# A two-layer decoder trunk: branch b's gate units computed in pairs, branch a's moved to the attention's end, one head pair's values kept in the rotary tables' tiles

## The chip, the cores and the metric

The kernel runs on one core of a Trainium2 chip. The metric is device time in microseconds (us) of one execution, as the median of a few runs. The core's engines are TensorE (PE, matmuls), VectorE (DVE), ScalarE (ACT), GpSimd (POOL) and SyncE (SP); POOL and SP issue most of the DMA transfers here. L12 is line 12 of the kernel.

## The reference

Each of two layers normalises the input, projects it to 6660 columns, runs three attention branches (a: forgetting attention, 4 heads; b: three dilated bands, 6 heads with rotary; c: a window of 128 with sinks, 6 query heads and 2 key heads with rotary), and merges them with gates:

```python
h = rmsnorm(x, norm_g[layer])
u = jnp.einsum('bsd,dc->bsc', h, w_in[layer])
(qa, ka, va, fa, za, qb, kb, vb, zb, qc, kc, vc, zc, ga, gb, gc) = jnp.split(u, offsets, axis=-1)
...
ya = ya.reshape(b, seq, A_W) * jax.nn.silu(za)        # and yb, yc likewise
...
merged = (jax.nn.sigmoid(ga) * jnp.einsum('bsc,cd->bsd', ya, w_br_a[layer])
          + jax.nn.sigmoid(gb) * jnp.einsum('bsc,cd->bsd', yb, w_br_b[layer])
          + jax.nn.sigmoid(gc) * jnp.einsum('bsc,cd->bsd', yc, w_br_c[layer]))
x = x + jnp.einsum('bsd,de->bse', merged, w_out[layer])
```

The sequence is 512 tokens, the model width 1024, a head 64 wide; a branch is 256 (a) or 384 (b, c) wide, two or three head pairs. A last normalisation follows.

## The kernel before

Activations lie as [128 channels x 512 tokens], weights stream from HBM. Every float32 operand is split in a high and a low part (`xh`, `xl`; `wh`, `wl`), and a product is three matmuls, high by high, high by low and low by high (`mm3`, L130 to L132). A weight chunk comes as a raw float32 tile, ACT makes or copies the parts (L1133, L1139), and a subtraction by DVE or POOL, or a DMA that accumulates (L1140), gives the low part.

**One layer** runs: value, query, key and z projections; an attention loop h = 0 to 16; a few gate units; input sums; pairs of gate units; the output projection (`o_item` in layer 0, `last_projection` in layer 1).

**The attention loop** issues, in iteration h: the transposes of head h-1 (`t_item`, L503), the units of slot a<h>, the value product of head h-1 (`pv_item`), the scores of head h+1 (`s_item`, L438 and L439), then the units of slot b<h>. The dictionary `plan` says which units stand in the slots. The products of scores and transposes go into four PSUM banks (`att`), given out in turn. For heads below 10 the scores take three banks and the transposes three; from head 10 on two and two. A bank of scores is read by the masked reduction on DVE (L472), a bank of transposes by ACT (L528) and DVE (L529). Rotary needs a swap of halves by a DMA from tile to tile on SP's queue; DVE waits for it at L353.

**A gate unit M(br, i)** (`m_item`, br 0, 1, 2 for branch a, b, c, i a block of 128 output channels) is the gate projection of its block (8 channel blocks, 24 matmuls of 512 columns) and the branch product (2 or 3 head pairs, 6 or 9 matmuls of 512 columns). Behind it DVE multiplies by the norm (L632), ACT takes tanh (L633), DVE multiplies gate and product (L639, L642) and, for b and c, adds it to the merged tile (L643).

**A pair** (`pair_steps`) computes two neighbouring gate units at once by a Strassen-Winograd scheme: seven products of a quarter (12 matmuls of 256 columns each; the products 2 to 5 by sums of inputs, `SH`, `SL`, and of raw weights), two branch products, and a chain of small operations (`e1`, `c11`, `e5`, `e2`, `c12`, `c22`, `c21`) that copies, adds, gates and merges the two units. The sums of the inputs are made once a layer at the attention's end (`sums_load` on SP's queue, L594; `sums`, L601 to L611); `x` is loaded again for it.

**Order.** A tile scheduler puts the instructions of each engine in order by priority, from the order in which the code gives them; `urgent` raises it. Instructions on one engine run in that order, and a DMA waits on its queue with all behind it. `raw_slots` names the tiles for the raw weights of the pairs: query and key tiles (`qk`, 12 buffers) up to pair (2,0), then y2 to y9. `y0` to `y9` hold the values of head pairs 0 to 5, two tiles each (pair 5 in y0 and y1 again); `va` tiles hold pairs 6 and 7. In layer 1 the last pair and the projection behind it stand in the order of the code.

## Time and profile before

| | us |
|---|---|
| three runs | 881.23, 884.04, 881.29 (median 881.29) |
| the profiled execution, own time | 884.22 |
| its span, first to last instruction | 882.5 |
| PE busy | 865.5 (98%) |
| DVE busy | 567.9 (64%) |
| ACT busy | 510.4 (58%) |
| POOL busy | 440.5 (50%) |
| layer 0: attention iterations 5 to 10 | 133.30 to 228.40 |
| layer 0: last value product ends, first pair starts | 282.2, 305.17 |
| layer 1: first pair starts | 736.10 |

The granted TensorE clock is 0.994 of full speed over the span. Busy shares are averages over the span; a busy PE is counted from the modelled ends of overlapping matmuls, so what a matmul costs is read from the distance of two starts.

### The profile page before, as it was taken

What the parts mean: (1) busy time and instruction counts of PE and PEld (TensorE: products, weight loads), DVE (VectorE), ACT (ScalarE), POOL (GpSimd) and SP (SyncE); (2) the same over time, 40 slices, a digit from 0 to 9 for tenths busy, and PEclk for the clock granted to TensorE, in tenths of its full rate; (3) what the DMA queues carried; (4) which work ended last, traced back from release to release, by engine and by line L of the source; (5) the groups of instructions that cost most, each with busy time, mean ns of one, the idle gap of its engine ahead of it and who ended that gap; (6) DMA issues with size and microseconds to landing.
All of it is one profiled execution on the core that took longest, in us unless ns stands there. A gap on an engine that the chain in (4) does not pass through costs nothing.

```text
span 882.5 us, 14401 instructions
## 1 busy us (share of the span) xinstructions
PE 865.5 (98%) x4866; PEld 750.1 (85%) x4866; DVE 567.9 (64%) x1242; ACT 510.4 (58%) x1072; POOL 440.5 (50%) x570
## 2 busy tenths in 40 slices
PE   9999999999999999999999999999999999999995
PEld 6988888888888889987888888888888888999994
DVE  7446788577576767752124658967685858687633
ACT  7477567565655655554335856666465756556541
POOL 5354576655444254566654446666444434544301
PEclk9999999999999999999999999999999999999997
DMA  9697768978989799999997886888899897998413
GB/s 303 142 207 141 161 142 168 190 144 189 199 182 228 193 185 247 205 200 284 250 233 156 174 164 149 153 168 172 158 205 193 186 223 158 226 247 183 160 48 111
DMA packets 97082, 163.83 MB, mean 186 GB/s; under 512 B 12144, under 2 KB 26864, under 8 KB 97008
## 3 DMA queue, kind: packets, MB, share of 16 engines
q0 software_dynamic: 71424, 121.70, 69.2%
q1 hardware_dynamic: 25440, 41.20, 14.2%
q8 instruction: 38, 0.62, 0.3%
q14 instruction: 36, 0.29, 0.1%
q10 hardware_dynamic: 144, 0.01, 0.0%
HBM read 153.43 MB, written 4.19 MB: 179 GB/s over the span
## 4 chain that ended last, share of the span: by engine, by line
PE 76%; issue 7%; POOL 5%; DMA 5%; DVE 3%; ACT 2%; SPq 0%; POOLq 0%; DVEq 0%; ACTq 0%
PE mm L131 17%; PE mm L130 17%; PE mm L132 17%; PE att L130 3%; PE att L131 3%; PE att L132 3%; PE pv L549 3%; PE att L503 3%; POOL wl L1140 3%; POOL wh L1110 2%; PE att L439 2%; PE att L438 2%; PE att L234 1%; PE att L235 1%; PE att L233 1%
## 5 line engine op out<-in xcount | busy, mean ns | idle before, releaser
L1140 POOL DMA_DIRECT2D wl<-in_wpk_dram x248 | 224.7, 925 | 185.8 <-ACT wl L1139 157.0
L1110 POOL DMA_DIRECT2D wh<-in_wpk_dram x248 | 169.6, 693 | 175.4 <-PE mm L132 130.2
L1139 ACT ACTIVATE wl<-wh 128x512 fp32r<-128x512 f32 (+3 forms) x248 | 148.3, 602 | 141.7 <-PE mm L132 113.2
L130 PE MATMUL mm<-xh,wh 128*128 128x512 f32 x544 | 217.6, 400 | 0.0
L131 PE MATMUL mm<-xl,wh 128*128 128x512 f32 x544 | 214.5, 394 | 0.0
L132 PE MATMUL mm<-xh,wl 128*128 128x512 f32 x544 | 214.4, 394 | 0.0
L132 PEld LDWEIGHTS mm<-xh,wl 128*128 128x128 f32 x544 | 102.2, 188 | 24.1
L130 PEld LDWEIGHTS mm<-xh,wh 128*128 128x128 f32 x544 | 102.3, 188 | 22.2
L131 PEld LDWEIGHTS mm<-xl,wh 128*128 128x128 f32 x544 | 102.3, 188 | 22.1
L474 ACT ACTIVATE P<-P,ng 128x256 f32<-128x256 f32 (+3 forms) x128 | 67.0, 525 | 24.9 <-DVE ng L472 24.4
L130 PE MATMUL mm<-y,wh 128*128 128x512 f32 (+1 forms) x132 | 49.9, 378 | 1.2 <-ACT y L711 1.2
L529 DVE TENSOR_TENSOR PL<-att,PH 128x512 fp32r<-128x512 f32 (+2 forms) x84 | 46.1, 598 | 7.0 <-ACT PH L528 7.0
L131 PE MATMUL mm<-y,wh 128*128 128x512 f32 (+1 forms) x132 | 50.1, 379 | 0.3 <-DVE y L712 0.3
L132 PE MATMUL mm<-y,wl 128*128 128x512 f32 (+1 forms) x124 | 47.5, 383 | 0.0
L130 PE MATMUL att<-xh,wh 128*128 128x256 f32 x144 | 40.7, 282 | 0.0
L492 DVE TENSOR_SCALAR P<-P,den 128x256 f32<-128x256 f32 (+3 forms) x128 | 39.8, 376 | 1.0
L132 PE MATMUL att<-xh,wl 128*128 128x256 f32 x144 | 40.4, 281 | 0.0
L131 PE MATMUL att<-xl,wh 128*128 128x256 f32 x144 | 40.4, 281 | 0.0
L528 ACT CAST PH<-att 128x512 fp32r<-128x512 f32 (+2 forms) x84 | 38.8, 526 | 1.3 <-PE att L503 0.6
L439 PE MATMUL att<-qk,qk 128*128 128x256 f32 (+2 forms) x128 | 36.9, 308 | 0.0
L503 PE MATMUL att<-ident,P 128*128 128x128 f32 x284 | 36.2, 272 | 0.0
L438 PE MATMUL att<-qk,qk 128*128 128x256 f32 (+2 forms) x128 | 36.1, 308 | 0.0
(260 smaller groups left out, 2034.8 us busy)
## 6 DMA issues: line engine op xcount, KB each, us to landing
wh<-in_wpk_dram POOLq DMA_DIRECT2D x196, 256.0 KB, 4.7
wl<-in_wpk_dram POOLq DMA_DIRECT2D x196, 256.0 KB, 5.2
y<-in_wpk_dram SPq DMA_DIRECT2D x32, 256.0 KB, 5.5
qk<-in_wpk_dram SPq DMA_DIRECT2D x24, 256.0 KB, 4.8
wh<-in_wpk_dram POOLq DMA_DIRECT2D x32, 192.0 KB, 5.0
wl<-in_wpk_dram POOLq DMA_DIRECT2D x32, 192.0 KB, 4.4
tmp<-tmp SPq DMA_DIRECT2D x80, 64.0 KB, 4.0
mg<-in_xT_dram SPq DMA_DIRECT2D x8, 256.0 KB, 5.7
```

Source lines behind the costliest of these rows:

```text
L130: nc.tensor.matmul(ps, wh, xh, start=first, stop=False, skip_group_check=part)
L131: nc.tensor.matmul(ps, wh, xl, start=False, stop=False, skip_group_check=part)
L132: nc.tensor.matmul(ps, wl, xh, start=False, stop=last, skip_group_check=part)
L438: nc.tensor.matmul(ps, q[:, qs], kh[:, a:a + n], start=True, stop=False)
L439: nc.tensor.matmul(ps, q2[:, qs], k2[:, a:a + n], start=False, stop=True)
L474: nc.scalar.activation(pb, pb, AF.Exp, bias=ng[:, i:i + 1], scale=-1.0, accum_out=den[:, i:i + 1])
L492: nc.vector.tensor_scalar(blks[i], blks[i], den[:, i:i + 1], None, op0=ALU.mult)
L503: nc.tensor.transpose(ps[:, c * P:(c + 1) * P], pt[:, src * P:(src + 1) * P], st["ident"])
L529: nc.vector.tensor_tensor(st["PL"][:, o:o + n], bk[:, :n], rd(hh), op=ALU.subtract)
L1110: nc.gpsimd.dma_start(hl[i][0][:, :w], ap)
L1139: nc.scalar.activation(lo[:, :w], rd(h[:, :w]), AF.Copy, scale=-1.0)
L1140: nc.gpsimd.dma_start(lo[:, :w], ap, accum_op=ALU.add)
```

## The change

- Slots of the attention: before, all eight units of branch a and M(1,0), M(1,1) stand in them, with M(1,2) and M(1,3) alone behind the loop. Now M(0,0) to M(0,5) stand in them, later than before, and M(0,6), M(0,7) behind the loop. Query and z projections of branch c change slots with them; b5, b7, b8 and b10 are empty.
- The pairs (1,0) and (1,2) come first in the list: eight pairs a layer instead of six. The small steps of every pair are urgent, where those of branch c alone were.
- The raw weights of five pairs, instead of three, come into query and key tiles, the first of them behind unit M(0,4).
- Branch a's units come later, so pair 0's values have to stay in y0 and y1: head pair 5's values go into the tiles of the rotary tables `cos` and `sin`, and `load_turns` loads the tables again when layer 0's output projection begins.
- In the last pair of a layer, the second unit's first 256 columns are normalised and gated one product earlier, and its merge is done in two halves. `last_projection` takes the merged units in natural order instead of `LATE` (7 before 6).

```diff
+    def load_turns():
+        st["cos"] = const(cos_d, [P, S], "cos")
+        st["sin"] = const(sin_d, [P, S], "sin")
...
             if pair < 6:
-                yh, yo = (y_slot((2 * pair + w) % 10) for w in range(2))
+                yh, yo = (y_slot(2 * pair + w) if pair < 5 else T([P, S], F32R, ("cos", "sin")[w]) for w in range(2))
...
-        now = urgent if br == 2 else (lambda fn: fn)
+        now = urgent
...
         def c12():
             nc.vector.tensor_tensor(d["g", 1][:, T0], d["b"], d["e"][:, T1], op=ALU.add)
+            if last:
+                norm(1, T0)()
+                gate(1, T0)()
 
         def c22():
             nc.vector.tensor_tensor(d["g", 1][:, T1], d["a"], d["e5"][:, T0], op=ALU.add)
-            norm(1, slice(0, S))()
-            gate(1, slice(0, S))()
+            c = T1 if last else slice(0, S)
+            norm(1, c)()
+            gate(1, c)()
...
-        do(now(merge(1, slice(0, S))))
+        if last:
+            do(now(merge(1, T0)), now(merge(1, T1)))
+        else:
+            do(now(merge(1, slice(0, S))))
...
-            for k in LATE:
+            for k in range(KT):
...
-            "b5": [(0, 0)],
-            "a6": [(0, 1)],
+            "b5": [],
+            "a6": [(0, 0)],
...
-        solo(M(1, 2))
+        solo(M(0, 6))
         do(sums(l, 1))
-        solo(M(1, 3))
-        for br, i in ((1, 4), (1, 6), (2, 0), (2, 2), (2, 4), (2, 6)):
+        solo(M(0, 7))
+        for br, i in ((1, 0), (1, 2), (1, 4), (1, 6), (2, 0), (2, 2), (2, 4), (2, 6)):
...
             o_item(0)
+            do(load_turns)
...
-                return ["qk"] * 4, ("p", key[1], 1, 0)
+                return ["qk"] * 4, ("p", key[1], 0, 4)
```

Of the slots, whose rows alone would tell little, this is what stands on PE where iteration 7 of layer 0 ends and iteration 8 begins. Before, the last matmuls of the unit in slot b7 (`mm_1983`), the transposes of head 7 into three banks, and the first of the z projection in slot a8 (`mm_2037`):

```order
L130 MATMUL mm_1983<-y_320_1515,wh_1665 128x512
L131 MATMUL mm_1983<-y_321_1516,wh_1665 128x512
L132 MATMUL mm_1983<-y_320_1515,wl_1754 128x512
L503 MATMUL att_1990<-ident_276,P_1774 128x128 x4
L503 MATMUL att_1991<-ident_276,P_1774 128x128 x4
L503 MATMUL att_1992<-ident_276,P_1774 128x128 x2
L130 MATMUL mm_2037<-xh_24_114,wh_1742 128x512
```

After, the last scores of head 8 (L442, L443), the transposes, and the z projection (`mm_1933`):

```order
L442 MATMUL att_1860<-qk_1637,qk_1526 128x512
L443 MATMUL att_1860<-qk_1638,qk_1526 128x512
L507 MATMUL att_1906<-ident_276,P_1722 128x128 x4
L507 MATMUL att_1907<-ident_276,P_1722 128x128 x4
L134 MATMUL mm_1933<-xh_24_114,wh_1500 128x512
L135 MATMUL mm_1933<-xl_25_115,wh_1500 128x512
L507 MATMUL att_1908<-ident_276,P_1722 128x128 x2
L136 MATMUL mm_1933<-xh_24_114,wl_1696 128x512
```

The transposes now follow the scores directly, with two matmuls of the next unit put between the second and the third bank.

On SP's queue, at the end of layer 0's attention, the last raw weights into query and key tiles, a load of the residual's tile (`sz`), two raw weights into y tiles, and the loads for the sums (L594) stood so before:

```order
L1105 DMA qk_3504<-in_wpk_dram 128x512
L769 DMA sz_4411<-in_xT_dram 128x512
L1105 DMA y_741_3679<-in_wpk_dram 128x512
L1105 DMA y_740_3677<-in_wpk_dram 128x512
L594 DMA tmp_2985<-in_xT_dram 128x512
L594 DMA tmp_2987<-in_xT_dram 128x512
```

And now (L598 are the sums' loads):

```order
L1117 DMA qk_3284<-in_wpk_dram 128x512
L598 DMA tmp_2777<-in_xT_dram 128x512
L598 DMA tmp_2779<-in_xT_dram 128x512
L780 DMA sz_4555<-in_xT_dram 128x512
L598 DMA tmp_2880<-in_xT_dram 128x512
L598 DMA tmp_2882<-in_xT_dram 128x512
L780 DMA sz_4557<-in_xT_dram 128x512
L598 DMA tmp_2901<-in_xT_dram 128x512
L598 DMA tmp_2903<-in_xT_dram 128x512
L598 DMA tmp_2956<-in_xT_dram 128x512
L598 DMA tmp_2958<-in_xT_dram 128x512
```

All eight loads for the sums now stand directly behind the query and key tiles; the two into y tiles have moved behind them.

On DVE, in the last pair of layer 1, the second unit (`tmp_8806`, merged tile `mg_7539`) was put together, normalised (L686), gated and merged (L699, L700, L712) so before; L1135 are low parts of the projection's weights:

```order
L734 TENSOR_TENSOR tmp_8806<-att_8829,tmp_8803 128x256
L1135 TENSOR_TENSOR wl_8926<-xh_1737_8862,wh_8864 128x512
L737 TENSOR_TENSOR tmp_8806<-att_8783,tmp_8804 128x256
L686 TENSOR_TENSOR tmp_8806<-tmp_8806,rbc_5113 128x512
L699 SCALAR_TENSOR_TENSOR tmp_8806<-tmp_8806,mm_8932 128x512
L700 TENSOR_TENSOR mg_7539<-mg_7539,tmp_8806 128x512
L712 TENSOR_TENSOR y_1758_8952<-mg_7539,y_1757_8951 128x512
```

And now (`tmp_9092`, `mg_7779`, lines four higher and more):

```order
L738 TENSOR_TENSOR tmp_9092<-att_9115,tmp_9089 128x256
L690 TENSOR_TENSOR tmp_9092<-tmp_9092,rbc_5261 128x256
L1147 TENSOR_TENSOR wl_9214<-xh_1791_9148,wh_9150 128x512
L744 TENSOR_TENSOR tmp_9092<-att_9069,tmp_9090 128x256
L690 TENSOR_TENSOR tmp_9092<-tmp_9092,rbc_5261 128x256
L703 SCALAR_TENSOR_TENSOR tmp_9092<-tmp_9092,mm_9220 128x256
L704 TENSOR_TENSOR mg_7779<-mg_7779,tmp_9092 128x256
L716 TENSOR_TENSOR y_1812_9240<-mg_7779,y_1811_9239 128x256
L703 SCALAR_TENSOR_TENSOR tmp_9092<-tmp_9092,mm_9220 128x256
L704 TENSOR_TENSOR mg_7779<-mg_7779,tmp_9092 128x256
L716 TENSOR_TENSOR y_1812_9240<-mg_7779,y_1811_9239 128x256
```

The unit is normalised and merged in two halves, the first half's norm ahead of the second half's sum.

## Rows read from the trace of the kernel before

**Rows 1.** The page, busy time by engine: us (share of the span), instructions.

```profile
PE 865.5 (98%) x4866; PEld 750.1 (85%) x4866; DVE 567.9 (64%) x1242; ACT 510.4 (58%) x1072; POOL 440.5 (50%) x570
```

**Rows 2.** Stretches: length, busy per engine (instructions), clock, DMA share, GB/s.

```profile
133.30:228.40 95.10, 95.10 (x476) 79.89 (x474) 69.14 (x162) 58.13 (x133) 55.63 (x68) 1.00 0.86 177
...
165.66:181.79 16.13, 16.13 (x81) 13.58 (x80) 10.04 (x24) 9.87 (x21) 12.14 (x13) 1.00 0.77 158
181.79:196.62 14.83, 14.83 (x76) 12.46 (x74) 11.46 (x27) 9.35 (x21) 6.67 (x10) 1.00 0.81 159
```

**Rows 3.** PE's timeline, unit M(1,2) and second pair: start, length, instruction [idle before].

```profile
289.85 0.40 PE L130 MATMUL mm<-xh,wh 128*128 128x512 f32 x1
...
297.52 0.39 PE L130 MATMUL mm<-xh,wh 128*128 128x512 f32 x1
...
319.61 0.28 PE L130 MATMUL att<-xh,wh 128*128 128x256 f32 x1
...
333.71 0.28 PE L130 MATMUL att<-xh,wh 128*128 128x256 f32 x1
```

**Rows 4.** Instruction groups by form, weight loads: busy us, mean ns of one.

```profile
L132 PEld LDWEIGHTS att<-xh,wl 128*128 128x128 f32 x144 | 27.1, 188 | 0.0
```

**Rows 5.** PE's timeline in attention: after scores (three places), and around the transposes.

```profile
142.52 0.39 PE L130 MATMUL mm<-xh,wh 128*128 128x512 f32 x1
...
165.66 1.25 PE L503 MATMUL att<-ident,P 128*128 128x128 f32 x10
166.67 0.48 PE L130 MATMUL mm<-xh,wh 128*128 128x512 f32 x1
...
174.89 0.39 PE L130 MATMUL mm<-xh,wh 128*128 128x512 f32 x1
...
605.59 0.39 PE L130 MATMUL mm<-xh,wh 128*128 128x512 f32 x1
```

**Rows 6.** DVE's timeline at the same places: the reductions L472.

```profile
143.12 0.41 DVE L472 CUSTOM_DVE_ANT_0 P<-att,mb 128x256 f32<-128x256 f32 x1
...
175.57 0.41 DVE L472 CUSTOM_DVE_ANT_0 P<-att,mb 128x256 f32<-128x256 f32 x1
...
176.62 0.54 DVE L472 CUSTOM_DVE_ANT_0 P<-att,mb 128x384 f32<-128x384 f32 x1
...
607.22 0.41 DVE L472 CUSTOM_DVE_ANT_0 P<-att,mb 128x256 f32<-128x256 f32 x1
...
608.16 0.54 DVE L472 CUSTOM_DVE_ANT_0 P<-att,mb 128x384 f32<-128x384 f32 x1
```

**Rows 7.** Instruction groups by form, a gate unit's norm: busy us, mean ns.

```profile
L632 DVE TENSOR_TENSOR tmp<-mm,rbc 128x512 f32<-128x512 f32 x24 | 16.4, 684 | 12.6 <-PE mm L132 12.6
```

**Rows 8.** DVE's waits from 133.30 to 228.40: us in total, times, longest.

```profile
DVE tmp L353 <- DMA tmp<-tmp: 8.6, 4, 3.8
DVE den L490 <- ACT P L474: 3.0, 5, 1.2
```

**Rows 9.** PE's timeline in the first pair of each layer.

```profile
311.10 0.39 PE L130 MATMUL att<-vb,wh 128*128 128x256 f32 x1 [1.50 <-ACT tmp L721]
...
741.49 0.39 PE L130 MATMUL att<-vb,wh 128*128 128x256 f32 x1 [1.33 <-ACT tmp L721]
```

**Rows 10.** SP's queue at the end of layer 0's attention: start, length, transfers.

```profile
271.84 0.80 SPq L1105 DMA_DIRECT2D y<-in_wpk_dram  x2
272.75 12.20 SPq L594 DMA_DIRECT2D tmp<-in_xT_dram  x4
```

**Rows 11.** PE's timeline where layer 1's last projection meets merged unit 7.

```profile
824.05 0.28 PE L132 MATMUL mm<-qk,wl 128*128 128x256 f32 x1
824.98 0.38 PE L130 MATMUL mm<-y,wh 128*128 128x256 f32 x1 [0.66 <-ACT y L711]
825.71 0.38 PE L131 MATMUL mm<-y,wh 128*128 128x256 f32 x1 [0.34 <-DVE y L712]
```

**Rows 12.** ACT's timeline where layer 0's output projection begins.

```profile
394.32 0.63 ACT L1139 ACTIVATE wl<-wh 128x512 fp32r<-128x512 f32 x1 [1.69 <-DMA wh<-in_wpk_dram]
```

More of the change, by code (lines that the diff above doesn't have):

```diff
@@ L813, in pe @@
                 mm3(ps, wh[:, c:c + P], wl[:, c:c + P], st["MH", k][:, tok], st["ML", k][:, tok],
-                    k == LATE[0], k == LATE[-1])
+                    k == 0, k == KT - 1)
             d["ps"] = ps
@@ L924, in layer @@
             "a5": [("kb", 2, 8)],
-            "b5": [(0, 0)],
-            "a6": [(0, 1)],
+            "b5": [],
+            "a6": [(0, 0)],
             "b6": [("kc", 0, 100)],
             "a7": [("qc", 0, 10)],
-            "b7": [(0, 2)],
+            "b7": [],
             "a8": [("zb", 2, 4)],
-            "b8": [("qc", 1, 12)],
-            "a9": [("qc", 2, 14)],
-            "b9": [(0, 3)],
-            "a10": [(0, 4)],
-            "b10": [("zc", 0, 5)],
-            "a11": [(0, 5)],
+            "b8": [],
+            "a9": [("qc", 1, 12)],
+            "b9": [("qc", 2, 14)],
+            "a10": [(0, 1)],
+            "b10": [],
+            "a11": [("zc", 0, 5)],
             "b11": [],
-            "a12": [(0, 6)],
+            "a12": [(0, 2)],
             "b12": [],
@@ L941, in layer @@
             "b13": [],
-            "a14": [("zc", 2, 7)],
+            "a14": [(0, 3)],
             "b14": [],
-            "a15": [(0, 7)],
+            "a15": [("zc", 2, 7)],
             "b15": [],
-            "a16": [(1, 0)],
-            "b16": [(1, 1)],
+            "a16": [(0, 4)],
+            "b16": [(0, 5)],
         }
@@ L1163, in load_consts @@
         st["ident"] = const(ident_d, [P, P], "ident")
-        st["cos"] = const(cos_d, [P, S], "cos")
-        st["sin"] = const(sin_d, [P, S], "sin")
+        load_turns()
         st["upper"] = const(upper_d, [P, P], "upper")
```

## Prediction

> **What bounds the kernel now.** I read the page's busy table first. TensorE (PE) is busy for 865.5 of 882.5 us [rows 1], so the time is the sum of PE's matmuls plus the few places where PE stands still. An edit can win only by giving PE less to do or by removing such a place, and it loses where it makes a new one. The table by stretches comes second, to see which engine is next in line: in iterations 5 to 10 of layer 0's attention (133.30 to 228.40) PE never stops, and the vector engine (DVE) is busy for 69.14 of 95.10 us [rows 2]. Third come PE's timeline, for what a matmul costs in each form, and then the waits, the chain and the queue of SP around PE's few gaps.
>
> The profiled run took 884.22 us with a span of 882.5, which leaves 1.7 us around it; the median of the three runs is 881.29, so 2.9 us below the profiled one. I make the sum as a difference and subtract it from both. About 0.3%, or 2.6 us, is what a measurement of this kernel can tell from no change.
>
> **1. Pairs in place of single units: -5.0 us.** Per layer four gate units of branch b leave the single form and become two pairs. A single unit of branch b is 33 matmuls of 512 columns (24 for the gate, 9 for the branch product) and takes 297.52 - 289.85 = 7.67 us from start to start [rows 3], 0.2325 us a matmul. A pair is seven products of 12 matmuls of 256 columns and two branch products of 9 matmuls of 512, and takes 333.71 - 319.61 = 14.10 us [rows 3]. Taking the 18 long ones off, 14.10 - 18 x 0.2325 = 9.92, the 84 short ones cost 0.118 each: half of a long one, so nothing is lost by the shorter form. Two units in single form are 15.34 us, a pair 14.10: 1.24 less, times two pairs and two layers, 4.96. Six pairs a layer run so already, with PE full between them, so I give this term no more than +-0.3.
>
> What could spoil it is the weight load: each matmul brings its own, and it shows as 188 ns busy [rows 4], more than the 118 ns that a short matmul takes. The rows say that the loads overlap, since 84 of them pass in 9.92 us. The Trainium skill, in "TensorE: Matmul & The Clock Gate", section "Back-to-back issue gap", gives sustained spacings of about 81 ns for 128 columns and 131 ns for 512, set by load and matmul together. By that a 256-column matmul would cost about three quarters of a 512-column one (an estimate between its two figures), a pair 18.8 us, and this term would be +14 us, a loss. The trace disagrees: a quarter product costs half here.
>
> **2. New stalls in attention: +4.0 us (bounds +1 and +10.7).** Iteration h puts on PE: the transposes of head h-1, the unit in slot a, the value product, the scores of head h+1, the unit in slot b. To make room for branch b's pairs, branch a's units move later, three projections with them, and the slots b5, b7, b8 and b10 become empty. Where b is empty, the transposes of the next iteration follow the scores at once. Below head 10 scores take three of the four attention banks and transposes three, so the second and third bank of the transposes wait until DVE's masked reductions (L472) have read the scores. Before, a unit of some 7 us stood between. From head 10 on both need two banks, so b10 costs nothing, as the empty slots b11 to b15 before.
>
> The price is the lag of DVE. Ten transposes take 166.67 - 165.66 = 1.01 us, so four are 0.4 [rows 5]. At iteration 5 the scores' last matmul is followed at 142.52 [rows 5] and the reduction of 256 columns that frees the first bank ends at 143.12 + 0.41 = 143.53 [rows 6], 1.0 later; the new order has four transposes and two matmuls of the next unit in front (0.4 + 0.47), so PE waits some 0.2. At iteration 7 PE goes on at 174.89 [rows 5] and the reductions end at 175.98 and 177.16 (starts 175.57 and 176.62 with 0.41 and 0.54) [rows 6]: 1.1 and 2.3 later. Here the new order has only the four transposes in front of the second bank (0.7 wait), then four more and two matmuls in front of the third (0.3): 1.0. In layer 1 the same place goes on at 605.59 [rows 5] with reductions ending at 607.63 and 608.70 [rows 6], 2.0 and 3.1 later: 1.6 + 0.2 = 1.8.
>
> The third place, iteration 8, depends on how late DVE is by then. Removing three units of branch a from iterations 5 to 10 takes 3 x 6.98 (30 matmuls of 0.2325) and one projection (24 matmuls) 5.58 from PE: 95.10 - 26.5 = 68.6 us. DVE loses two operations over 512 columns for each, L632 at 684 ns [rows 7] and a second that I take alike: 4 x 1.37 = 5.5, so about 64 of 68.6 us are left, 93%, where it was 73%. In iterations 7 and 8 PE keeps 9.2 us of work each (transposes 1.0, a 24-matmul projection 5.6, value product and scores about 2.6), while DVE needs 10.04 and 11.46 - 1.37 = 10.1 [rows 2]: DVE falls behind by about 1.7 us, less the 1.0 that the stall before gives back. I take 1.0 for layer 0 and nothing for layer 1, where the larger stall ahead has let DVE catch up. Sum: 0.2 + 1.0 + 1.0 in layer 0, 1.8 in layer 1, 4.0. The lower bound has DVE as prompt as at iteration 5 everywhere (0.2 x 6, about 1). The upper one keeps all of DVE's waits for the rotary swap, 8.6 us in this stretch [rows 8], beside its 64 us of work: 72.6 against 68.6, 4.0 a layer, and 1.3 a layer for the lag at the three places: 10.7.
>
> **3. The first pair's stall: -2.4 us (bounds -2.8 and +2).** In the first pair of each layer PE waits 1.50 and 1.33 us for ScalarE's copy of product a (L721) [rows 9]. The chain behind it starts on SP's queue. The loads for the input sums (L594, issued at 272.75) stand behind two weight loads into y3 and y2 (271.84) [rows 10], which may go only when the last branch-a unit has read those tiles. That makes the sums late, one after the other, and the gates between them on the same engines, up to the copy. Now all loads for sums stand ahead of y3 and y2 on the queue, so the first ones go when their tiles are free, some 2.5 us earlier, and with them the chain. Against that, three single units of 6.98 (20.9 us) stand between the last value product and the first pair, where three of 7.67 (23.0) stood: the need is 2 us earlier too. But each branch-a unit has one DVE operation less behind it (no addition into the merged sum, 0.6 us each), and the copy is now urgent. Net I expect 0.2 to 0.3 us of wait to stay per layer: 2 x 1.2 won. If the sums come no earlier, the wait grows by the 2 us of a layer, less 0.6 to 1: that is the +2.
>
> **4. The end: -1.4 us (bounds -1.4 and -0.7).** The last projection of layer 1 meets two gaps: its first matmul with merged unit 7 starts at 824.98 instead of 0.12 after 824.05, the second at 825.71 instead of 0.12 after 824.98 [rows 11]: 0.81 + 0.61. They wait for the cast and the remainder of that unit, whose 512 columns are gated and merged in one go. Now its first half has norm and gate one product earlier and its merge works on 256 columns. The natural order puts it last in the projection. PE has product 6 (1.4) and 21 matmuls of 0.118 (2.5) in front of it, and the chain of four operations on 256 columns, at some 0.41 each as the reduction of that size [rows 6], takes 1.6: both gaps go.
>
> **5. The rotary tables' reload: +0.6 us (bounds -0.5 and +2).** Head pair 5's values now stand in the tiles of the cosine and sine tables, and 512 KB are loaded again on SP's queue as layer 0's output projection begins. The queue gets two entries that wait for the last pair's branch product; the residual loads stand behind them. The memory traffic comes where ScalarE already waited 1.69 us for weights at 394.32 [rows 12], so a part of a microsecond is likely; two loads in a row of this size would be the worst. The tables are next read in layer 1's attention, so the loads themselves are hidden; the values are written after the last rotary projection, so that write waits for nothing. The raw weights of two more pairs pass through the twelve query and key tiles on the same queue: each set has two pairs, 28 us, to arrive, so I take 0.
>
> **Sum.** -5.0 + 4.0 - 2.4 - 1.4 + 0.6 = -4.2 us: the profiled run 884.2 - 4.2 = 880.0, the median 881.3 - 4.2 = 877.1; I say 877.0.
>
> **Rivals.** *A, the gain is eaten.* The first pair's stall stays (term 3 is 0), because the copy still waits for a gate of the unit ahead, and iteration 8 stalls longer: -5.0 + 5 + 0 - 1.4 + 0.6 = -0.8, 880.5. For it: the chain into 311.10 has many links, and one that stays late is enough. Against: its first link, the queue order, is plainly changed. *B, slower: DVE becomes the bound of iterations 5 to 9.* At 93% busy its in-order waits no longer fit beside its work. If both large kinds stay whole, for the rotary swap (8.6) and for the exponentials (3.0) [rows 8], its path is 64 + 11.6 = 75.6 us against PE's 68.6: 7.0 a layer, 14.0 in place of 4.0, 887. It decides against the change from a path of some 74 us, where 5.4 a layer brings the sum to 883.9. For it: the reductions that free the banks stand behind such a wait in the order of DVE. Against: part of these waits is there because DVE came early, and a late DVE finds the swap landed. *C, short matmuls bound by weight loads*: 84 x 0.188 + 4.2 = 20.0 us a pair, +18.6, 900. The six pairs of before rule it out almost wholly. *D, the pairs don't replace the units*: the new list has eight pairs and the plan no unit of branch b, so I leave it no chance.
>
> **Chances.** Forecast (874 to 878.6) 0.52, rival A (878.7 to 883.9) 0.28, rival B 0.19, C 0.01. All of the forecast is faster by over 0.3% (below 878.65), A is within, B and C above 883.9. The low end, 873, takes the best of terms 2 to 5 in part (-5.0 + 1.5 - 2.8 - 1.4 - 0.5 = -8.2); the high end, 884.5, leaves out most of B.
>
> **What would show it.** After: 28.2 us between the starts of the first and third pair, less the first's stall; PE waits on DVE's L476 (L472 before) in front of the transposes of iterations 6, 8 and 9 adding up to about 4 us, none in front of iteration 11; L721's successor L725 with under 0.6 us of wait in each first pair; no gap in the first last_projection units. Wrong would be: attention longer than its matmuls by more than 6 us, a first-pair wait over 1.5, or SP's queue held by the table loads.

## The result: 1.7% slower

| | us |
|---|---|
| before, median of 4 runs | 881.57 (881.23 to 884.04) |
| after, median of 4 runs | 897.76 (893.05 to 900.07) |
| ratio | 1.0171, 95% interval 1.0156 to 1.0187 |
| the profiled execution of after, own time and span | 899.07 and 897.3 |

The forecast was 877.0, with 873.0 to 884.5 as its range, so the sign was wrong and the time lies far outside. Of the rivals two ended slower. C, at 900, is nearest by its number, but not by its cause: a pair still costs 14.1 us (below), so the short matmuls aren't bound by their weight loads. B, at 887, had DVE run out of time in the attention; the traces show that DVE had time left, though one remark of B's came true: the reductions that free the banks stand behind DVE's wait for a rotary swap.

### The profile page after: what moved, and what is told of

It is laid out like the page before. It is cut to its first block, busy times and chain, and to the rows that moved or that the text cites. A ratio compares the mean times of both kernels' runs of the same rounds, so it can differ in the third digit from the quotient of the medians.

```text
span 897.3 us, 14818 instructions
## 1 busy us (share of the span) xinstructions
PE 866.5 (97%) x5010; PEld 755.6 (84%) x5010; DVE 589.4 (66%) x1298; ACT 519.6 (58%) x1100; POOL 434.1 (48%) x562
## 4 chain that ended last, share of the span: by engine, by line
PE 69%; DMA 13%; DVE 8%; issue 4%; ACT 2%; SPq 2%; POOL 1%; DVEq 0%; POOLq 0%; ACTq 0%
PE mm L134 14%; PE mm L136 14%; PE mm L135 14%; PE att L134 5%; PE att L136 5%; PE att L135 5%; DMA tmp<-tmp 4%; DMA qk<-in_wpk_dram 2%; PE pv L553 2%; PE att L507 2%; DMA wl<-in_wpk_dram 2%; PE att L443 1%; PE att L442 1%; SPq L352 1%; PE att L238 1%
## 5 line engine op out<-in xcount | busy, mean ns | idle before, releaser
L134 PE MATMUL mm<-xh,wh 128*128 128x512 f32 x480 | 192.7, 402 | 0.0
L136 PE MATMUL mm<-xh,wl 128*128 128x512 f32 x480 | 190.3, 396 | 0.0
L135 PE MATMUL mm<-xl,wh 128*128 128x512 f32 x480 | 189.4, 395 | 0.0
L136 PEld LDWEIGHTS mm<-xh,wl 128*128 128x128 f32 x480 | 90.4, 188 | 20.7
L134 PEld LDWEIGHTS mm<-xh,wh 128*128 128x128 f32 x480 | 90.6, 189 | 18.9
L134 PE MATMUL att<-xh,wh 128*128 128x256 f32 x192 | 54.2, 282 | 3.3 <-DVE tmp L744 3.3
L136 PE MATMUL att<-xh,wl 128*128 128x256 f32 x192 | 53.9, 281 | 0.0
L135 PE MATMUL att<-xl,wh 128*128 128x256 f32 x192 | 53.9, 281 | 0.0
L507 PE MATMUL att<-ident,P 128*128 128x128 f32 x284 | 38.9, 277 | 8.1 <-DVE ng L476 6.0
L134 PE MATMUL mm<-y,wh 128*128 128x512 f32 (+1 forms) x116 | 44.1, 380 | 0.8 <-ACT y L715 0.8
L507 PEld LDWEIGHTS att<-ident,P 128*128 128x128 f32 x284 | 32.9, 142 | 13.9 <-issue 7.8
L1131 DVE TENSOR_TENSOR qk<-qk,qk 128x512 f32<-128x512 f32 x40 | 27.6, 691 | 21.9 <-DMA qk<-in_wpk_dram 21.2
L136 PE MATMUL mm<-y,wl 128*128 128x512 f32 (+1 forms) x108 | 41.4, 384 | 0.0
L134 PEld LDWEIGHTS att<-xh,wh 128*128 128x128 f32 x192 | 36.2, 188 | 5.3 <-DVE tmp L744 4.6
L134 PE MATMUL att<-vb,wh 128*128 128x256 f32 x128 | 36.3, 284 | 3.7 <-ACT tmp L725 3.6
```

The source lines that it names most:

```text
L134: nc.tensor.matmul(ps, wh, xh, start=first, stop=False, skip_group_check=part)
L135: nc.tensor.matmul(ps, wh, xl, start=False, stop=False, skip_group_check=part)
L136: nc.tensor.matmul(ps, wl, xh, start=False, stop=last, skip_group_check=part)
L507: nc.tensor.transpose(ps[:, c * P:(c + 1) * P], pt[:, src * P:(src + 1) * P], st["ident"])
L1131: nc.vector.tensor_tensor(o, a, b, op=ALU.subtract)
```

## The profile after

The busy row of the page, to be held against [rows 1], and PE's waits over the whole span (us in total, times, longest):

```profile
PE 866.5 (97%) x5010; PEld 755.6 (84%) x5010; DVE 589.4 (66%) x1298; ACT 519.6 (58%) x1100; POOL 434.1 (48%) x562
```

```profile
PE att L507 <- DVE ng L476: 6.0, 5, 2.6
PE att L134 <- ACT tmp L725: 3.6, 2, 1.9
PE att L134 <- DVE tmp L744: 3.3, 3, 1.2
PE att L507 <- DVE P L496: 2.1, 2, 1.4
PE att L443 <- DVE qk L379: 1.6, 2, 1.0
...
PE att L136 <- DMA wl<-in_wpk_dram: 1.3, 2, 0.8
```

Of these six only the second had a like in the trace of before, L721 with 1.50 and 1.33 us [rows 9]. L507 are the transposes, L443 scores, L134 and L136 in `att` the pairs' quarter products. PE has less to do than before and yet shows 1.0 us more busy time; a part of that is the clock (last section), and the ends of overlapping matmuls are modelled.

Where the time went is read best by stage. The table gives the length of each, from the starts in PE's timeline (layer 1's first pair of before starts at 735.75, not at 736.10 as the table ahead of the prediction has it); "expected" is what the prediction's own PE work gives without a new wait.

| stage | before | after | change | expected |
|---|---|---|---|---|
| layer 0: iterations 1 to 4 | 59.27 | 60.46 | +1.2 | 0 |
| iterations 5 to 10 | 95.10 | 72.31 | -22.8 | -26.5 |
| iterations 11 to 16 | 53.80 | 52.46 | -1.3 | -2.1 |
| single units behind the loop | 22.97 | 20.90 | -2.1 | -2.1 |
| pairs | 86.54 | 117.00 | +30.5 | +28.2 - 1.2 |
| output projection to layer 1's attention | 112.97 | 113.73 | +0.8 | +0.6 |
| layer 1: iterations 1 to 4 | 59.30 | 60.10 | +0.8 | 0 |
| iterations 5 to 10 | 95.06 | 73.59 | -21.5 | -26.5 |
| iterations 11 to 16 | 53.73 | 53.25 | -0.5 | -2.1 |
| single units | 22.98 | 20.87 | -2.1 | -2.1 |
| pairs | 86.30 | 120.54 | +34.2 | +28.2 - 1.2 |
| last projection, to the last matmul | 51.24 | 49.53 | -1.7 | -1.4 |

The sum of the changes is +15.5 us, the difference of the spans 14.8. The stretches behind the loss, as the table of stretches gives them for after (length, busy per engine with instructions, granted clock, DMA share, GB/s):

```profile
134.59:206.90 72.31, 69.47 (x361) 58.05 (x360) 56.36 (x135) 46.80 (x107) 40.11 (x47) 1.00 0.77 156
206.90:259.36 52.46, 51.78 (x287) 44.52 (x285) 40.96 (x115) 35.60 (x91) 21.15 (x30) 1.00 0.88 201
280.26:397.26 117.00, 113.55 (x817) 106.43 (x816) 82.05 (x148) 61.81 (x123) 60.80 (x86) 1.00 0.96 207
571.09:644.68 73.59, 70.46 (x361) 59.30 (x360) 56.87 (x136) 47.51 (x109) 40.24 (x47) 0.98 0.76 158
...
718.80:839.34 120.54, 115.68 (x817) 107.82 (x816) 84.78 (x150) 62.01 (x125) 54.48 (x75) 0.99 0.92 207
```

Look at DVE in iterations 5 to 10: 56.36 of 72.31 us, 78%. The prediction had it at 93%. DVE is not out of time there; PE waits for it all the same.

Two groups of waits carry the loss. **In the attention**, the transposes behind an empty slot wait for the masked reductions, in layer 0 at the three places that were forecast (iterations 6, 8 and 9), in layer 1 at the first two of them, and those of iteration 16 wait for the scaled scores (PE's timeline; the bracket is the wait):

```profile
145.16 0.85 PE L507 MATMUL att<-ident,P 128*128 128x128 f32 x6 [0.28 <-DVE ng L476]
...
172.03 0.63 PE L507 MATMUL att<-ident,P 128*128 128x128 f32 x4 [1.74 <-DVE ng L476]
...
182.94 0.63 PE L507 MATMUL att<-ident,P 128*128 128x128 f32 x4 [0.81 <-DVE ng L476]
...
250.66 0.95 PE L507 MATMUL att<-ident,P 128*128 128x128 f32 x7 [0.68 <-DVE P L496]
...
609.72 1.09 PE L507 MATMUL att<-ident,P 128*128 128x128 f32 x4 [2.62 <-DVE ng L476]
```

DVE's own timeline a moment earlier shows what it did: nothing. It stood at the rotary swap in flight, once in each layer, and the reductions are behind it in its order. From the landing to the end of the one that frees the second bank (L476 over 256 columns) DVE then works for 3.4 us, in both layers (before, 3.4 in layer 0 and 4.6 in layer 1):

```profile
168.47 0.69 DVE L357 TENSOR_TENSOR tmp<-tmp,sin 128x512 f32<-128x512 f32 x1 [4.90 <-DMA tmp<-tmp]
...
171.46 0.41 DVE L476 CUSTOM_DVE_ANT_0 P<-att,mb 128x256 f32<-128x256 f32 x1
```

```profile
606.16 0.69 DVE L357 TENSOR_TENSOR tmp<-tmp,sin 128x512 f32<-128x512 f32 x1 [4.92 <-DMA tmp<-tmp]
```

**In the first two pairs**, PE waits for the pair's small steps:

```profile
288.96 0.39 PE L136 MATMUL att<-vb,wl 128*128 128x256 f32 x1 [0.55 <-DMA wl<-in_wpk_dram]
...
295.12 0.39 PE L134 MATMUL att<-xh,wh 128*128 128x256 f32 x1 [1.23 <-DVE tmp L744]
...
302.74 0.39 PE L134 MATMUL att<-vb,wh 128*128 128x256 f32 x1 [1.68 <-ACT tmp L725]
```

And DVE, in the same stretch, stands at L1131, the difference of raw weights for the fourth and fifth pair, while the steps of the first two stand behind it; SP's queue shows that these weights were issued late, when tiles came free:

```profile
290.45 0.69 DVE L1131 TENSOR_TENSOR qk<-qk,qk 128x512 f32<-128x512 f32 x1 [3.17 <-DMA qk<-in_wpk_dram]
...
300.13 0.69 DVE L1131 TENSOR_TENSOR qk<-qk,qk 128x512 f32<-128x512 f32 x1 [2.95 <-DMA qk<-in_wpk_dram]
300.74 0.68 DVE L704 TENSOR_TENSOR mg<-mg,tmp 128x512 f32<-128x512 f32 x1
301.35 0.42 DVE L750 TENSOR_TENSOR tmp<-att,rbc 128x256 f32<-128x256 f32 x1
```

```profile
283.26 11.83 SPq L1117 DMA_DIRECT2D qk<-in_wpk_dram  x4
```

L750 at 301.35 is followed on ACT by the gate and then by L725, for which PE waits until 302.74.

## The experiments

Twelve kernels, e1 to e12, in three batches, each beside its own runs of before. The ratio is to before. After stands at 897.76 us and 1.0171, and in its second measurement (e10) at 899.84 and 1.0187; where a kernel is compared with after, both differences are given. Before's own median was 881.57, 881.76, 882.74 and 882.86 in the four measurements, so a difference of some 1 us between batches tells nothing. One trace tells little more: iterations 5 to 10 of layer 0, with the same instructions in the same order on every engine, took 72.25 to 74.95 us in the six traces of after, e10, e1, e2, e3 and e4.

**Attention or pairs?** The first two keep the new slots and take pairs away. e1 has six pairs:

```diff
         solo(M(0, 7))
-        for br, i in ((1, 0), (1, 2), (1, 4), (1, 6), (2, 0), (2, 2), (2, 4), (2, 6)):
+        for i in range(4):
+            solo(M(1, i))
+        for br, i in ((1, 4), (1, 6), (2, 0), (2, 2), (2, 4), (2, 6)):
```

> The changed kernel, but with six pairs a layer: the units (1,0) to (1,3) run alone behind M(0,7), as 33 matmuls of 512 columns each. The slots of the attention stay as changed. Theory 'attention and first pairs both lose': PE has 4 x 1.24 = 5.0 us more to do than in the changed kernel, but the first pair comes 30.7 us a layer later, with all sums and raw weights landed, so the waits of about 3.9 and 4.9 us in the first two pairs go: net about -4, near 893, and PE's waits in the attention (L507, L443) stay at about 10 us. Rival 'the attention alone loses it': the first pairs' waits are small in other executions; the time goes up by 5 to about 902. Rival 'the pairs lose it': the attention's waits in the changed kernel's one trace are chance, and the time falls to about 883.

Measured: 892.26, ratio 1.0114 (1.0086 to 1.0143). Iterations 5 to 10 took 72.25 and 71.68 us, waits on L476 came to 5.1 us, on L496 to 2.1 (some 10 were expected). No wait is left in the first pairs. With PE's extra 5.0 us in it, it is still 5.5 and 7.6 us faster than after. So the first theory holds: the attention loses by itself, and the first pairs lose more than the pairs give. e2 has seven pairs:

```diff
         solo(M(0, 7))
-        for br, i in ((1, 0), (1, 2), (1, 4), (1, 6), (2, 0), (2, 2), (2, 4), (2, 6)):
+        for i in range(2):
+            solo(M(1, i))
+        for br, i in ((1, 2), (1, 4), (1, 6), (2, 0), (2, 2), (2, 4), (2, 6)):
```

> The changed kernel, but with seven pairs a layer: M(1,0) and M(1,1) run alone behind M(0,7), and pair (1,2) comes first. Theory 'the first pairs start before sums and raw weights are there': 15.3 us a layer more of cover take most of the first pairs' waits away (3.9 and 4.9 us to under 1 each), for 2 x 1.24 us of PE work: about -5, near 893. Rival 'they are late by a queue, not by time': the waits come back in the new first pairs, and the time goes up by 2.5.

Measured: 890.61, ratio 1.0098 (1.0072 to 1.0124), 7.2 and 9.2 us faster than after. Layer 0's seven pairs took 98.84 us with no wait in them, 14.1 a pair; in layer 1 one wait of 1.1 us on L725 was left in the new first pair. So most of the loss goes when the first pair comes later: the first pairs started before their inputs were ready.

**Which input?** In e3 a zero, made from the first copy of the pair before, is read by the subtractions of the fourth and later pairs, so that DVE can't come to them early:

```diff
+            z = T([P, 1], F32, "zz", 2)
+            nc.vector.tensor_scalar(z, d["e"][:, 0:1], 0.0, None, op0=ALU.mult)
+            st["zz", l, br, i] = z
...
-        nc.vector.tensor_tensor(o, a, b, op=ALU.subtract)
+        n = PAIRS.index(key[2:4])
+        if n >= 3 and key[4] in (2, 3):
+            z = st[("zz", key[1]) + tuple(PAIRS[n - 1])]
+            nc.vector.scalar_tensor_tensor(o, a, z, b, op0=ALU.add, op1=ALU.subtract)
+        else:
+            nc.vector.tensor_tensor(o, a, b, op=ALU.subtract)
```

> The changed kernel; the subtractions of raw weights for products 2 and 3 of the fourth and later pairs read one zero that is made from the first copy of the pair before them, so they can't stand earlier than that in DVE's order. Theory 'DVE stands in its order at raw weights that are still in flight (3.17 us at 290.45, 2.95 at 300.13) while the pair in hand waits behind': these waits go, PE's waits on L744 and L725 in the first two pairs fall from about 3 us a layer to under 1.5, time -3 to -5, about 893. Rival 'the sums and ACT's queue are late anyway': the waits move to another releaser and the time stays within 1.5 us.

Measured: 894.48, ratio 1.0141 (1.0103 to 1.0179). The interval touches those of after, so the time alone is no proof; the trace is clear. DVE's waits for raw weights:

```profile
DVE qk L1139 <- DMA qk<-in_wpk_dram: 7.6, 4, 2.4
```

They were 21.2 us in ten places for qk tiles and 7.4 in eight for y tiles in after; no wait for y tiles is left. PE's wait on L744 in the first pair and on L725 in the second, 1.23 and 1.68 us in layer 0 and 0.88 and 1.87 in layer 1, went in both layers. What stayed is one wait of 1.64 on L725 in the first pair of layer 0, two of 0.92 and 0.48 for a weight DMA, and the one at the end. The pairs took 115.96 and 115.29 us, against 117.0 and 120.5 in the trace of after and 118.2 and 118.2 in its second. Eight pairs without a wait would take 112.7 (six in 84.5, as e9 has them, and two of 14.1). So by these traces DVE's standing at raw weights is about half of the pair stage's loss. The wait of iteration 16 looks to be of the same kind: in after DVE stands at L1131, at the third pair's raw weights, with the scaling of head 15 (L496) behind it. There e3 holds nothing back, and PE still waits 0.92 and 1.40; no run holds that difference back, so this one is argued from the order alone.

```profile
248.09 0.69 DVE L1131 TENSOR_TENSOR qk<-qk,qk 128x512 f32<-128x512 f32 x1 [1.66 <-DMA qk<-in_wpk_dram]
...
249.45 1.07 DVE L496 TENSOR_SCALAR P<-P,den 128x128 f32<-128x128 f32 x4
```

**Urgency.** e4 takes it from branch b's pairs:

```diff
-        now = urgent
+        now = urgent if br == 2 else (lambda fn: fn)
```

> The changed kernel with urgent small steps in branch c's pairs alone, as before the change. Theory 'urgency has no part in the loss': within 1.5 us of the changed kernel. Rival 'urgent steps push the splits of the next products back on DVE and ACT': 3 us faster.

Measured: 901.27, ratio 1.0213 (1.0187 to 1.0238): slower than after by 3.5 and 1.4 us. Its interval touches the first of after and overlaps the second, so it can't be told to be slower; faster it is not. The rival falls: urgency is no part of the loss.

**The swap.** In e5 the rotary term's DMA is left out:

```diff
-        for a, b in ((0, 32), (32, 0), (64, 96), (96, 64)):
-            nc.sync.dma_start(sw[a:a + 32, :], x[b:b + 32, :])
...
-        nc.vector.tensor_tensor(sw, sw, st["sin"], op=ALU.mult)
+        sw, x = sw
+        nc.vector.tensor_tensor(sw, x, st["sin"], op=ALU.mult)
```

> The changed kernel without the DMA that swaps the halves for the rotary term: DVE multiplies the unswapped tile by the sine table, so the result of that term is wrong, and 80 small transfers and DVE's waits for them are left out. The changed kernel needs 72.3 and 73.6 us for iterations 5 to 10, against 68.6 of matmuls. Theory 'DVE is late because it stands at swaps in flight': 69 to 70.5 in both layers, PE's waits on L476 at most 2 of 6 us, time -6 to -8, near 890. Rival 'the order of the banks alone, with DVE as prompt as it can be': 71 and more, time -2 to -3.

Measured: 893.96, ratio 1.0122 (1.0104 to 1.014), 3.8 and 5.9 us better than after. Iterations 5 to 10: 70.94 and 71.02 us. No wait on L476 is left at all, but the scheduler has put DVE's work in another order, and the value product waits instead:

```profile
PE pv L552 <- DVE PL L532: 3.5, 2, 1.8
PE att L506 <- DVE P L495: 3.2, 2, 1.7
```

So the waits on the banks go when the swap goes. But the order of DVE's work changed with it, and length and time lie between what the two theories gave (69 to 70.5 against 71 and more; -6 to -8 against -2 to -3): the run doesn't separate the swap from the order. Its time also holds a stretch at half the clock in the output projection (402.2 to 405.5, last section). How short these iterations would be without a swap and in the old order stays open.

**Another empty slot.** e6 empties b9 in place of b8:

```diff
-            "b8": [],
+            "b8": [("qc", 2, 14)],
...
-            "b9": [("qc", 2, 14)],
+            "b9": [],
```

> The changed kernel with the projection of branch c's third query pair in slot b8 and not b9: b9 is empty in place of b8. The transposes at iteration 9 then have 5.6 us behind the scores, those at iteration 10 follow scores of two banks. Theory 'a bank wait costs only where the scores hold three banks': the wait at iteration 9 (about 1.0 and 0.3 us) goes and one of at most 0.5 comes at iteration 10; time 0 to -2. Rival 'DVE is short of time in iterations 7 to 9 however the slots stand': the stall moves one iteration on and the time stays.

Measured: 904.06, ratio 1.0239 (1.0216 to 1.0263), 6.3 and 4.2 us slower than after. The wait of iteration 9 went, as expected, and waits of 1.20 and 0.58 us came at iteration 10, on the third bank alone. That was expected at 0.5 at most. The waits of iteration 8 were 2.80 and 3.07 us, and the granted clock was 0.51 in four stretches (304.5 to 308.0, 406.9 to 410.4, 615.1 to 622.0 and 744.8 to 748.3), 17 us together, where after's trace has 7. That is up to 5 us more, of the 7.4 by which this trace's execution (906.51, the longest of its four) is longer than after's. The other three took 901.57 to 904.52. Both theories fall short of it.

**Slots filled again.** e7 has slots as before up to b8, M(0,7) in b16, M(1,0) and M(1,1) alone, seven pairs (added lines only, against after):

```diff
...
+            "b5": [(0, 0)],
+            "a6": [(0, 1)],
...
+            "b7": [(0, 2)],
...
+            "b8": [("qc", 1, 12)],
+            "a9": [("qc", 2, 14)],
+            "b9": [],
+            "a10": [(0, 3)],
...
+            "b16": [(0, 7)],
```

> Slots nearly as before the change (b5, b7, b8 filled; only b9 and b10 empty), seven units of branch a in the attention, M(0,7) in b16, M(1,0) and M(1,1) alone behind the loop, then seven pairs a layer; the rest as changed. Theory 'the empty slots below head 10 and the early first pair are the loss': iterations 5 to 10 have no wait on L476 but one of at most 1 us at iteration 10, the first pair's stall is like before's (1.7 and 1.5 us) or less, and the two pairs more than before give 2.5 us: 878 to 881, at or just under the kernel before. Rival 'the traffic of more raw weights and the table reload cost time themselves': 884 and more.

Measured: 888.89, ratio 1.007 (1.0055 to 1.0085): 8.9 and 11.0 us better than after, and still slower than before. The three places are free of waits. The one empty slot b9 costs 1.63 and 1.31 us at iteration 10, iteration 16 waits 0.86 and 0.89 on L496, the pairs some 1.5 to 3 us, and the end 1.3. Two pairs give 2.5 us, and these waits take more. The 878 to 881 of the first theory is missed, and the time lies in the rival's range; yet the trace has waits enough for it, and e11 below finds no price of the table reload. So the first theory named the right places, but not all of them.

**One empty slot by itself.** e12 is the kernel before, with one unit moved from b7 to b10; PE's work is the same:

```diff
-            "b7": [(0, 2)],
+            "b7": [],
...
-            "b10": [("zc", 0, 5)],
+            "b10": [("zc", 0, 5), (0, 2)],
```

> The kernel before with slot b7 empty: its unit M(0,2) stands in slot b10 behind the z projection that was there, so PE has the same work and nothing else moves. The changed kernel's trace has 1.9 and 3.5 us of wait at iteration 8. Theory 'an empty slot below head 10 costs the lag of DVE behind the scores': a wait on L472 of 1 to 3 us a layer at iteration 8 alone, time +2 to +6. Rival 'the changed kernel waits there since DVE has lost its slack over several iterations': under 0.5 us a layer, time within 1 of before.

Measured: 887.84, ratio 1.0054 (1.0033 to 1.0076), +5.0 us. PE's timeline and two stretches of layer 1:

```profile
177.81 0.63 PE L503 MATMUL att<-ident,P 128*128 128x128 f32 x4 [1.03 <-DVE ng L472]
```

```profile
608.79 0.63 PE L503 MATMUL att<-ident,P 128*128 128x128 f32 x4 [2.05 <-DVE ng L472]
```

```profile
606.00:609.00 3.00, 0.95 (x8) 0.64 (x7) 2.88 (x8) 2.17 (x4) 1.59 (x1) 1.00 0.99 178
...
610.50:613.50 3.00, 3.00 (x9) 2.32 (x8) 1.73 (x6) 2.95 (x8) 1.71 (x2) 0.50 0.08 19
```

The whole of iterations 5 to 10 grew by 1.34 us in layer 0 and by 4.06 in layer 1. PE and DVE have before's work here, so the first theory holds: the wait belongs to the slot. The two waits, 1.03 and 2.05 us, are close to what the prediction read for this place from before, 1.0 and 1.8. In layer 1 nearly half of the price isn't the wait: behind it the granted clock was 0.50 for some 3 us.

**The end.** e8 has the edits of the last pair and the natural order, on the kernel before:

```diff
+            if last:
+                norm(1, T0)()
+                gate(1, T0)()
...
-            norm(1, slice(0, S))()
-            gate(1, slice(0, S))()
+            c = T1 if last else slice(0, S)
+            norm(1, c)()
+            gate(1, c)()
...
+        if last:
+            do(now(merge(1, T0)), now(merge(1, T1)))
...
-            for k in LATE:
+            for k in range(KT):
```

> The kernel before with the edits of the last pair and the natural order in the last projection alone. Theory of the prediction: both gaps of 0.81 and 0.61 us go, -1.4. Rival, from the changed kernel's trace, where product 6 of the last pair waits 1.4 us on DVE (L744), which stands behind a late weight load: the gaps are traded for that one, within 0.7 us of before.

Measured: 881.15, ratio 0.998 (0.9967 to 0.9994), 1.6 us under its runs of before. By the time alone the first theory would stand; the trace shows what the rival named: both old gaps are gone, and product 6 of the last pair waits 1.3 us on L740. What gave the time all the same isn't shown. In after it is the same, on L744; DVE's and PE's timelines there:

```profile
834.39 1.34 DVE L690 TENSOR_TENSOR tmp<-tmp,rbc 128x256 f32<-128x256 f32 x1
836.73 0.69 DVE L1147 TENSOR_TENSOR wl<-xh,wh 128x512 fp32r<-128x512 f32 x1 [0.99 <-DMA xh<-in_wpk_dram]
837.34 0.42 DVE L744 TENSOR_TENSOR tmp<-att,tmp 128x256 f32<-128x256 f32 x1
```

```profile
837.81 0.39 PE L134 MATMUL att<-xh,wh 128*128 128x256 f32 x1 [1.24 <-DVE tmp L744]
```

The early norm (L690) and a weight's low part (L1147), which waits for its load, stand in front of L744, which frees the bank. e9 splits norm, gate and merge just so, but all behind that sum (the split of the merge and the natural order as in e8):

```diff
-            norm(1, slice(0, S))()
-            gate(1, slice(0, S))()
+            for c in (T0, T1) if last else (slice(0, S),):
+                norm(1, c)()
+                gate(1, c)()
...
```

> The kernel before with the second unit of the last pair normalised, gated and merged in two halves, but all of it behind the second half's sum, and the natural order in the last projection. Theory 'the early norm and gate put DVE and ACT behind a weight cast, so product 6 of the last pair waits 1.45 us; without it the split merge alone closes the old gaps of 0.81 and 0.61': -1.4 against before, and no wait of product 6. Rival 'the merge in halves comes too late too': the gap at merged unit 7 stays above 0.5 us, time within 0.7 of before.

Measured: 880.53, ratio 0.9968 (0.9957 to 0.998): faster than before, by 0.3% or 2.3 us, and the fastest of all here; of these the theory explains 1.4. Neither the old gaps nor the new wait are in its trace. Its pairs took 84.47 and 84.72 us, with no wait in the first pair.

**The tables.** e11 is the kernel before with this edit alone (`load_turns` as in the change):

```diff
...
-                yh, yo = (y_slot((2 * pair + w) % 10) for w in range(2))
+                yh, yo = (y_slot(2 * pair + w) if pair < 5 else T([P, S], F32R, ("cos", "sin")[w]) for w in range(2))
...
             o_item(0)
+            do(load_turns)
```

> The kernel before with head pair 5's values in the tiles of the rotary tables and the tables loaded again when layer 0's output projection begins, nothing else. The prediction's term 5 says +0.6 us (-0.5 to +2), at the start of that projection. Rival 'the reload costs nothing, what the changed kernel lost there is the clock and the merge': within 0.5 us of before.

Measured: 883.44, ratio 1.0005 (0.9991 to 1.0019): no difference that can be told. In its trace the stage from the output projection on is 1.0 us longer than before's, in waits for merged tiles at 395.19 to 397.14, which fits the +0.6 as well as it fits 0.

**After once more.** e10 is the changed kernel without an edit.

> The changed kernel again, for a second trace beside the other kernels of this batch. Theory 'its waits have their place, their lengths vary with the landing of DMAs': the same places wait (L476 at iterations 6, 8 and 9, L496 at iteration 16, L744 and L725 in the first two pairs, L744 at the end), iterations 5 to 10 take 72 to 74 us in both layers, time 893 to 900. Rival 'one odd execution': some of these places don't wait.

Measured: 899.84, ratio 1.0187 (1.0158 to 1.0215). The same places wait. Iterations 5 to 10 took 73.44 and 73.97 us, 11 to 16 took 53.31 and 53.84, the pairs 118.19 and 118.24. The lengths vary: iteration 8 of layer 0 waits 2.62 us here and 1.74 in the first trace, and the first pairs wait 0.75 and 0.69 on L725, where the first trace has none.

## Why the prediction was wrong, step by step

**Term 1, the pairs' saving (-5.0): right.** A pair costs 14.1 us, as six of them did before and as the seven of the second experiment do: the seventh adds at most 98.84 - 84.47 = 14.4. The spacings that the Trainium skill gives ("TensorE: Matmul & The Clock Gate", "Back-to-back issue gap": about 81 ns for 128 columns, 131 for 512) would, by the prediction's estimate from them, have made it a loss; the traces disagree, with 0.2325 us for 512 columns and 0.118 for 256.

**Term 2, stalls in attention (+4.0): right in kind and for three places, mis-sized.** The stage table gives 3.7 + 0.8 us for layer 0 and 5.0 + 1.6 for layer 1, 11.1 together (14.0 in the second trace), above the upper bound of 10.7. In the 11.1 the brackets on L476 are 6.0 us, those on L496 2.1, and half the clock behind the wait of 2.62 us took some 1.4. Most of the rest is that a bracket begins at the modelled end of the matmul before it: each of these seven waits is some 0.2 longer from start to start.

The reading of the lag was sound for the kernel that it was taken from, as e12's waits show. Three things were missed. First, the landing came later against PE. At iteration 7 it stood 2.3 and 2.5 us ahead of the end of the scores in before, and 1.2 and 0.3 in after. PE's work from the transposes to the scores is the same there, 7.9 us. But DVE came to the product that the swap copies (L341, L345 in after) 0.2 us behind the start of the transposes in before, where it had waited for PE, and 0.6 and 1.8 us in after; and the swap took 6.6 and 6.4 us from its first issue, where it was 5.9 and 5.7. DVE's timeline in layer 1, before and after, where the transposes start at 596.37 and 597.27 and the scores end at 605.59 and 606.50:

```profile
596.57 0.69 DVE L341 TENSOR_TENSOR tmp<-mm,rbc 128x512 f32<-128x512 f32 x1 [0.79 <-PE mm L132]
...
603.07 0.70 DVE L353 TENSOR_TENSOR tmp<-tmp,sin 128x512 f32<-128x512 f32 x1 [3.60 <-DMA tmp<-tmp]
```

```profile
599.03 0.69 DVE L345 TENSOR_TENSOR tmp<-mm,rbc 128x512 f32<-128x512 f32 x1
```

Second, iteration 16 wasn't on the list: DVE stood there at raw weights of the third pair. Third, some of the waits are followed by a stretch at half the clock, which no term has.

The bound above it, and rival B, rested on DVE's work, 64 of 68.6 us. That was the wrong measure. DVE was busy for 56.36 of 72.31, since more than the gate units' operations left that stretch: one head's reductions and scaling (24 of L496 in place of 28 of L492) and 1.4 us of raw weights' differences. DVE had 16 us to spare there, and PE waited for it by where it stood in its order.

**Term 3, the first pair's stall (-2.4): wrong in sign, the largest error.** The step on the queue was right: the last four of the sums' loads were issued from 262.36 on, 3.0 us behind the end of the last value product, where it was 5.6. Two other steps failed. First, "2 x 1.2 won" took [rows 9] for a property of the kernel. In the traces of e8 and e9, which have the same instructions up to layer 0's first pair, and of e11, no first pair waits at all; in e12 they wait 1.0 us together. The 1.50 and 1.33 us of wait were that one execution's, 2.8 together, and they are about what it had over the median, 2.9 us. The prediction saw that difference and subtracted the gain from both. The wait for the copy is gone from the first pairs of after's first trace, but there was as good as nothing to win by it. Second, "each set has two pairs, 28 us, to arrive, so I take 0" looked at when the weights are used and not at where DVE is made to wait for them. The scheduler put the differences of the fourth and fifth pair into DVE's order during the first two, the tiles came free only then, and DVE stood there with the pair in hand behind it. The pairs' stage lost 4.3 us in layer 0 and 7.8 in layer 1 against the 112.7 without waits: 12.1, of which 1.2 is the new wait at the end and some 1.7 the clock behind the wait of 1.87 us. e3 shows DVE's standing to be about half of it; the rest goes, too, when the first pair comes later (e1, e2), and which input it is then stays open.

**Term 4, the end (-1.4): half right.** The gaps went, and a new wait of the same size came, since the early norm, with a weight's low part behind it, was put in front of the sum that frees a bank. The kernel that does it behind the sum has the gain.

**Term 5, the tables (+0.6): within what can be told**, +0.8 in the trace of after and no difference in the time of the edit alone.

Iterations 1 to 4, with the same instructions in the same order up to there, took 1.2 and 0.8 us longer in the trace of after. In other traces here layer 0's took 59.3 to 61.7, and where they were long, PE mostly waited on L443 or L439 behind a swap that landed late: DVE stood at it for 5.85 us in after (until 97.91) and for 3.80 in before. That is a difference of executions.

Together, from the trace of before to that of after: -5.0 for the pairs' work, +11.1 in the attention, +12.1 in the pairs' stage, less the 3.8 that this stage had lost in before's own trace, +0.8 at the output projection, +2.0 in iterations 1 to 4 and -1.7 at the end are the +15.5 of the stage table.

What is not settled is how the later landing in the attention divides between DVE's order and the flight of the swap, and why e6's other executions are slower than after, beyond the clock in its trace.

## What to carry to other kernels

A unit of work that seems to fill time can be the cover of an in-order engine's waits; before it is taken away, list what that engine stands at there, and how far each landing is from the use, not how busy the engine is. When transfers move closer together, look at where in each engine's order their first reader stands and who is behind it. Before a gap is booked as a gain, see that it is in more than one execution; a profiled run that is slower than the median by about that gap is a warning.

## What the hardware showed that was not expected

After some waits PE ran at half the clock for some 3 us, 1.2 of 2.4 GHz. In e12 the granted clock was 0.50 from 610.50 to 613.50, after PE had been busy for 0.95 of the 3.00 us up to 609. In after there are two such stretches, behind the waits of 2.62 and 1.87 us in layer 1:

```profile
609.00:612.50 3.50, 2.79 (x10) 2.42 (x11) 3.02 (x11) 3.41 (x10) 3.35 (x3) 0.51 0.40 95
742.20:745.60 3.40, 3.40 (x15) 3.11 (x14) 2.53 (x5) 2.62 (x6) 2.38 (x4) 0.50 0.72 142
```

There a 512-column matmul took 0.43 us from start to start, at 744.09, 744.51 and 744.94, where it is 0.23 otherwise. A PE at half clock counts as busy, so the page's busy time hides it. Half of such a stretch is lost, so after's two cost some 3 us of the 15. Not every wait does it, and its length doesn't decide: behind 1.74 us in layer 0 of after and 2.62 in layer 0 of e10 the clock stayed at 1.00, and in e1 two waits of 0.80 and 0.50 us in the output projection were followed by 0.50 from 401.6 to 405.0. What a wait costs can so be twice its own length and more, and the difference is found only in the granted clock of the stretch behind it.
